# Rows 256 to 511 enter the first projection unscaled, and the scan's tables are asked for later

## The chip, the cores and the metric

The kernel runs on one core of a Trainium2 chip. A core has a matrix engine (PE in the profile), a vector engine (DVE), a scalar engine (ACT), a general engine (POOL) and a queue that mostly issues transfers (SP). Each takes its own instructions strictly in order; they meet through semaphores. The metric is the device time of one execution in microseconds (us). Executions of one kernel mostly agree within 0.3 per cent.

## What is computed

One layer of a hybrid encoder over 2048 rows of width 1024, all in float32:

```python
hn = rmsnorm(h, mix_norm_g)                       # per row: x * rsqrt(mean(x*x) + eps) * g
u, g_ssm, q, k, v, g_attn = split(hn @ w_in, 6)   # six times 512 columns
y_ssm = s5_branch(u, ...) * silu(g_ssm)           # diagonal complex scan, GELU, GLU
y_att = stick_breaking_branch(q, k, v, ...) * silu(g_attn)
h = h + concat([y_ssm, y_att]) @ w_out
h = h + sigmoid(rmsnorm(h) @ w_ple_gate) * (p @ w_ple_proj)
```

The reciprocal root of a row (its scale) is one number per row. It can be put on x before the product, or on the product behind it.

## The kernel before

Products keep float32 accuracy: each operand is split into a high and a low part (`split`, lines 505 to 508: ACT writes `hi`, DVE writes `lo = src - hi`), and three matmuls are made for each pair of blocks (`mm3`, lines 530 to 537).

The first phase (`phase_u`, line 540) makes u transposed: channels on partitions, rows along the free axis. It takes the rows in eight steps T of 256. A step needs `xt`, the transposed and split x, and the eight split blocks `w` of `w_in`'s first 512 columns; it makes 4 column tiles by 8 blocks by 3 = 96 matmuls of 128x256, into four banks `ps_u`.

- T = 0 (`load_plain`, line 546) reads a copy of x that the host has laid out transposed, so no transposes are needed and the scale isn't known when the products start. For each of four pairs of blocks, two transfers of 128 KB (one for each 128 rows), two splits, and two blocks of w (256 KB each, `load_w`, line 467, hi on ACT at line 485, lo on DVE at line 488) are asked for. `norms` (line 567) squares x in place on ACT, adds on POOL (line 571), sums over partitions with a matmul against ones (line 573), takes the power on POOL, and spreads the scale along the free axis as `e.row` with another matmul (line 579). The result in `ps_u` is multiplied by that row on DVE as it leaves the bank (line 627).
- T = 1 to 7 (`load_x`, line 582): the rows are loaded plainly, squared on ACT with a sum (line 590), the scale is worked out on DVE and POOL (`rms_rstd`, line 497), x is multiplied by it on ACT (line 592), transposed by PE into two banks `ps_x` (16 small transposes of 64x64 for each 128 rows), and split into `xt`. The result leaves `ps_u` by an ACT copy (line 629).

Every `xt` is also stored (`hn_d`), and the gate units (`gate_unit`, line 636) and the attention's projections (`attn_proj`, line 706) read it. Where it is unscaled (T = 0, rows 0 to 255) they multiply their products by the row's scale (`e.row` or `e.rs[i]`).

Beside this phase, `ssm_chain` (line 176) works out the scan's tables: a long string of small DVE instructions (`ex_`, `sc_`, `pr_`, `cm`, `tabs`, `pw`, `bb` in the profile). Its inputs come in seven transfers that POOL issues (lines 196, 198 and 205). `ssm_pack` (line 307) makes weights from them, four POOL and DVE instructions at a time; the first matmuls that use them come after the last step of u.

Nothing runs in program order. `arrange` (line 1525) takes all instructions with their dependencies, times them with a model of its own (`duration`, `list_schedule`), and writes out a fixed order for every engine, the best of six turns. Hints enter here: `e.first()` puts a group ahead, `e.mark(k)` names an instruction, and `e.later(k)` keeps a transfer in that plan behind the marked instruction. Any change thus renews the order of all engines over the whole kernel.

Tiles with one tag share a ring of buffers: `x` has four, `uq` (the results of u, and three of w's raw blocks ahead of them) has four.

Of the kernel before, what the change touches and what calls it, by code (L numbers as in the profile page):

```python
# [18 lines left out]
P = 128  # L19
# [30 lines left out]
HOLD = 2  # L50
ACT0 = True
MARK0, MARK1 = 7, 6
MATB = 1
# [122 lines left out]
def ssm_chain(e, keep, sm):  # L176
# [15 lines left out]

    dma = e.cdma
    ldt, lr, li = t("ldt"), t("lr"), t("li")
    for d, name in ((ldt, "log_dt"), (lr, "a_re"), (li, "a_im")):
        dma(d, e.small(name))
    dsk = R.dsk = kt("dsk", [G])
    dma(dsk[96:], e.small("d")[96:])

    bst = sm.tile([P, G, GH], F32, tag="bst", name="bst")  # L200
    bsw = sm.tile([P, G, GH], F32, tag="bsw", name="bsw")
    R.cts = kt("cts", [G, GH])
    R.ct2 = kt("ct2", [G, GH])
    for d, name in ((bst, "b"), (bsw, "b_turned"), (R.cts, "c"), (R.ct2, "c_turned")):
        dma(d, e.small(name).rearrange("p (g h) -> p g h", g=G))
    vs(nc, R.cts, R.cts, sgn, ALU.mult)
# [92 lines left out]
    for o, src, n in ((dec1, rho, KIN), (dec2, t1, MOUT), (tabs[:, :, NTAB - 1:].rearrange("p g n -> p n g"), rho, 1)):  # L299
        nc.vector.tensor_copy(o, src.unsqueeze(1).to_broadcast([P, n, G]))  # L300
        if n > 1:
            nc.vector.memset(o[:, 0], 0.0)
    dma(e.tb_d, tabs)
    return R
# [162 lines left out]
def load_w(e, blocks, width, scale, tag="w", pool=None, bufs=None, at=0, act=True, spare=None):  # L467

    nc = e.nc
    out = []  # L470
    for c, src in enumerate(blocks, at):
        t = (pool or e.wpool).tile([P, 2, width], F32R, tag=tag, name=f"w_{tag}", **({"bufs": bufs} if bufs else {}))
        hi, lo = t[:, 0], t[:, 1]
        if spare is None or c < STB + STA:
            raw = e.stage[c % len(e.stage)].tile([P, 512], F32, tag="wst", name="wst")[:, :width]
        else:
            raw = spare.tile([P, L, NCH // 2], F32, tag="uq", name="wst", bufs=4).rearrange("p j c -> p (j c)")[:, :width]
        if c == MARK0 and spare is not None:
            e.mark(0)
        e.wdma(raw.rearrange("p (k c) -> p k c", k=src.shape[1]) if len(src.shape) == 3 and src.shape[0] == P else raw, src)  # L480
        if scale is None:
            split(e, hi, lo, raw)
        else:
            if act:
                nc.scalar.activation(hi, raw, AF.Copy, scale=scale[:, c:c + 1])  # L485
# [54 lines left out]
def phase_u(e, pool, xp, chain):  # L540
# [5 lines left out]
    def load_plain(T):  # L546
        xt = xp.tile([P, 2, 2, NC8, P], F32R, tag="xg", name="xt", bufs=2)
        w = []
        for hf in range(2):
            plain.append(pool.tile([P, NC8, P], F32, tag="x", name="x", bufs=XB))  # L550
        for c in range(0, NC8, 2):
            cs = slice(c, c + 2)
            for hf in range(2):
                x = plain[2 * T + hf]
                nc.sync.dma_start(x[:, cs], e.xt[2 * T + hf, :, cs])
                split(e, xt[:, hf, 0, cs], xt[:, hf, 1, cs], x[:, cs])
            if T == 0:
# [8 lines left out]

    def norms(i):
        x, r = plain[i], e.rs[i]
        nc.scalar.activation(x, x, AF.Square)
        for n in (4, 2, 1):  # L570
            nc.gpsimd.tensor_tensor(x[:, :n], x[:, :n], x[:, n:2 * n], op=ALU.add)
        ps = e.bank("ps_row", "tr", "ssm")
        nc.tensor.matmul(ps[:, :1], x[:, 0], ones[:, :1], start=True, stop=True)
        vs(nc, r, ps[:, :1], 1.0 / DM, ALU.mult, EPS, ALU.add)
        nc.gpsimd.tensor_tensor(r, r, e.mhalf[:, :1], op=ALU.pow)
# [3 lines left out]
        nc.tensor.matmul(ps[:, :P], ones, d, start=True, stop=True)  # L579
        nc.scalar.activation(e.row[i // 2][:, i % 2 * P:i % 2 * P + P], ps[:, :P], AF.Copy)  # L580

    def load_x(T):
        xt = xp.tile([P, 2, 2, NC8, P], F32R, tag="xg", name="xt", bufs=2)
        for hf in range(2):
# [5 lines left out]
            nc.scalar.activation(jk, x, AF.Square, accum_out=ss)  # L590
            rs = rms_rstd(e, pool, ss, 1, DM, "x")
            nc.scalar.activation(x, x, AF.Copy, scale=rs)
            for h, ps in enumerate(turned(e, "ps_x", ("z0", "z1"), [x[:, c * P:(c + 1) * P] for c in range(NC8)])):
# [6 lines left out]
    with e.first():  # L600
        xts[0], w = load_plain(0)
        norms(0)
        norms(1)
        with e.later(0):
            xts[1] = load_x(1)
    prep = chain()
    for T in range(NT // 2):
# [4 lines left out]
        if T % 4 == 0:  # L612
            uq = [pool.tile([P, L, NCH // 2], F32, tag="uq", name="uq", bufs=4) for ct in range(4)]
        ps = [e.bank("ps_u", "w0", "w1", "o", "acc", *(("z0", "z1") if T < 1 else ()))[:, :256] for _ in range(4)]
        if T == 2:
            e.mark(T)
        for ct, c in [(ct, c) for c in range(NC8) for ct in range(4)] if T == 0 else [(ct, c) for ct in range(4) for c in range(NC8)]:
            if T == 0 and ct == 0 and c == MARK1:
# [4 lines left out]
        for ct in range(4):  # L623
            k0 = (T % 4) * n
            o, out = ps[ct].rearrange("p (c j) -> p j c", j=L), uq[ct][:, :, k0:k0 + n]
            if T < 1:
                vt(nc, out, o, e.row[T].rearrange("p (c j) -> p j c", j=L), ALU.mult)
            else:
                nc.scalar.activation(out, o, AF.Copy)
            if T % 4 == 3:  # L630
# [5 lines left out]
def gate_unit(e, pool, w, T, xt):  # L636
# [6 lines left out]
    for ct in range(4):  # L643
        o = e.bank("ps_sg", "o", "z0", "z1")[:, :256]
        for c in range(NC8):
            cs = slice(ct * P, (ct + 1) * P)
            mm3(e, o, (w[c][:, 0, cs], w[c][:, 1, cs]), (xt[:, :, 0, c], xt[:, :, 1, c]), c == 0, c == NC8 - 1)
        if T < 1:
            og = pool.tile([P, 256], F32, tag="sg", name="og", bufs=2)
# [56 lines left out]
def attn_proj(e, pool, A, i, xt=None):  # L706
# [8 lines left out]
    if len(e.q_banks) == 1:  # L715
        pq = e.bank("ps_qk", *e.q_banks)
        for c in range(NC8):
            mm3x(e, pq, (xt[:, 0, c], xt[:, 1, c]), (A.w[c][:, 0], A.w[c][:, 1]), c == 0, c == NC8 - 1)
        if i < 2:
            nc.scalar.activation(flat, pq[:, :384], AF.Copy, scale=e.rs[i])  # L720
# [4 lines left out]
    else:  # L725
# [7 lines left out]
        part = pool.tile([P, 512], F32, tag="part", name="part", bufs=1)  # L733
        if i < 2:
            nc.scalar.activation(part, pq[0], AF.Copy, scale=e.rs[i])
# [291 lines left out]
def hybrid_block_kernel(ctx: ExitStack, tc: tile.TileContext, x, xt, small, p, w_in, ssm_w_glu, w_out, w_ple_gate,  # L1027
# [36 lines left out]
    nc.vector.memset(e.mhalf, -0.5)  # L1064
    e.rs = [const(f"rs{i}", [P, 1]) for i in range(2)]

    def part(name):
        at = 0
        for q, n in SMALL:
            if q == name:  # L1070
                return small[:, at:at + n]
            at += n
# [10 lines left out]
    def late_consts():  # L1083
# [3 lines left out]
        gk = column("gk", 1)  # L1087
        vt(nc, e.gqk, e.gqk, gk, ALU.mult)

# [49 lines left out]
    gx = pool(left, "gx")  # L1139
    e.row = [gx.tile([P, 256], F32, tag=f"row{T}", name=f"row{T}") for T in range(1)]  # L1140
    early = ExitStack()
# [443 lines left out]
```

## Time and profile before

| | |
|---|---|
| three runs | 1561.94, 1563.83 and 4259.91 us |
| median | 1563.83 us |
| profiled execution | 1561.94 us, of which the span of the instructions is 1560.2 us |
| mean granted PE clock | 0.984 |
| instructions | 34921 |
| busy, share of the span | PE 95%, DVE 69%, ACT 60%, POOL 53% |

In a row of a timeline the columns are the start, the duration, the engine, the source line, the operation, `out<-in` with the names of the tiles, the shape and the count; in brackets stands how long the engine sat idle before it and what released it. In a row of a table by windows stand the window, its length, and then for each engine the busy time and the number of instructions, at the end the granted PE clock, the share of the DMA engines' time, and GB/s.

### The profile page before, as it was taken

Reading aid. Unit: us, or ns where it says so; the run is one execution under the profiler, and the core shown is the slowest. Engines: PE = TensorE matmul, PEld = TensorE weight load, DVE = VectorE, ACT = ScalarE, POOL = GpSimd, SP = SyncE. Lnnn points to the kernel's source line nnn. Section 1 sums busy time; section 2 is a strip of 40 time slices with the busy share of each in tenths; the row PEclk is TensorE's granted clock in tenths of the full one; section 3 lists DMA queues with packets and bytes.
Section 4 is the critical chain, followed back from the end, with each engine's and each line's share of the span. In section 5 each row is a group of like instructions: output and inputs, shape, how many; then the busy total and the mean of one; then the engine's idle time right before and its main releaser. Section 6 shows DMA issues by size and latency. Waiting matters only on the chain.

```text
span 1560.2 us, 34921 instructions
## 1 busy us (share of the span) xinstructions
PE 1480.4 (95%) x13116; PEld 1257.4 (81%) x13116; DVE 1073.6 (69%) x2052; ACT 938.7 (60%) x2076; POOL 819.2 (53%) x1038
## 2 busy tenths in 40 slices
PE   5999999999999999998999988999998999999998
PEld 5999999978888788887887876777776888777776
DVE  8944868867667876778867776666869556754444
ACT  5654445557577877677777777766765435633432
POOL 3241433445455665565656688765565654433433
PEclk8999999999999989999999988999999999999999
DMA  8777735565332412234323466763448645612211
GB/s 294 272 250 222 237 119 188 165 198 163 116 116 99 150 67 98 105 116 128 99 94 112 138 213 180 220 184 93 112 136 257 199 161 183 200 63 94 89 62 61
DMA packets 168969, 236.21 MB, mean 151 GB/s; under 512 B 63664, under 2 KB 110816, under 8 KB 157408
## 3 DMA queue, kind: packets, MB, share of 16 engines
q1 hardware_dynamic: 166416, 225.38, 44.7%
q0 software_dynamic: 2384, 8.59, 2.0%
q8 instruction: 104, 1.70, 0.4%
q14 instruction: 65, 0.53, 0.1%
HBM read 169.03 MB, written 64.90 MB: 150 GB/s over the span
## 4 chain that ended last, share of the span: by engine, by line
PE 74%; DVE 9%; ACT 5%; issue 4%; DMA 4%; POOL 3%; POOLq 0%; SPq 0%; ACTq 0%; DVEq 0%
PE ps_q L732 19%; PE ps_o L836 6%; PE ps_z L797 5%; PE ps_wt L520 4%; PE ps_g L701 3%; PE ps_g L703 3%; PE ps_g L702 3%; PE ps_h L702 3%; PE ps_h L703 3%; PE ps_h L701 3%; DVE px L813 2%; PE ps_sg L535 2%; PE ps_sg L536 2%; PE ps_sg L537 2%; DMA wst<-in_ssm_w_glu_dram 2%
## 5 line engine op out<-in xcount | busy, mean ns | idle before, releaser
L815 POOL TENSOR_TENSOR be<-be,px 128x512 f32<-128x512 f32 (+3 forms) x320 | 317.6, 998 | 224.3 <-DVE px L813 177.1
L813 DVE TENSOR_TENSOR_SCAN px<-px,ps_z 128x512 f32<-128x512 f32 (+3 forms) x320 | 340.2, 1086 | 108.6 <-ACT be L807 81.8
L732 PE MATMUL ps_q<-w_w,xt 64*128 64x512 f32 x2880 | 400.9, 404 | 6.6 <-DVE v L65 3.6
L732 PEld LDWEIGHTS ps_q<-w_w,xt 64*128 64x128 f32 x2880 | 294.5, 187 | 43.8 <-PE ps_z L797 7.2
L828 ACT ACTIVATE ws<-ps_wt 128x512 f32<-128x512 f32 (+3 forms) x320 | 165.0, 547 | 76.2 <-PE ps_wt L520 75.9
L802 ACT ACTIVATE px<-ps_z 128x512 f32<-128x512 f32 (+3 forms) x320 | 162.4, 538 | 67.6 <-PE ps_z L797 48.7
L807 ACT ACTIVATE be<-ps_z 128x512 f32<-128x512 f32 (+3 forms) x320 | 168.7, 554 | 1.3 <-PE ps_wt L520 1.2
L797 PE MATMUL ps_z<-k,q 64*128 64x512 f32 (+3 forms) x960 | 146.3, 385 | 15.9 <-DVE px L813 12.4
L836 PE MATMUL ps_o<-ws,v 128*64 128x128 f32 x2176 | 139.8, 281 | 0.9 <-ACT ws L828 0.9
L836 PEld LDWEIGHTS ps_o<-ws,v 128*64 128x64 f32 x2176 | 121.0, 140 | 19.1 <-issue 15.5
L520 PEld LDWEIGHTS ps_wt<-ident,be 64*128 64x128 f32 x2176 | 101.1, 142 | 36.6 <-issue 15.3
L797 PEld LDWEIGHTS ps_z<-k,q 64*128 64x128 f32 x960 | 94.9, 189 | 35.0 <-DVE px L813 18.2
L520 PE MATMUL ps_wt<-ident,be 64*128 64x64 f32 x2176 | 108.5, 229 | 13.4 <-POOL be L815 4.8
L1008 POOL TENSOR_TENSOR sg<-sg,h 128x512 f32<-128x512 f32 x32 | 44.9, 1414 | 114.6 <-DVE sg L65 114.6
L501 POOL TENSOR_TENSOR rs_qk<-rs_qk,mhalf 128x4 f32<-128x4 f32 x64 | 66.6, 1040 | 39.7 <-DVE rs_qk L72 38.8
L535 PE MATMUL ps_u<-xt,w_w 128*128 128x256 f32 x256 | 74.8, 294 | 8.1 <-ACT w_w L485 7.0
L65 DVE TENSOR_TENSOR yr<-sx,yr 128x512 fp32r<-128x512 f32 x64 | 53.6, 858 | 34.6 <-ACT yr L507 33.7
L537 PE MATMUL ps_u<-xt,w_w 128*128 128x256 f32 x256 | 74.3, 296 | 3.0 <-DVE w_w L76 3.0
L536 PE MATMUL ps_u<-xt,w_w 128*128 128x256 f32 x256 | 74.8, 293 | 0.7 <-DVE xt L65 0.7
L507 ACT ACTIVATE yr<-sx 128x512 fp32r<-128x512 f32 x64 | 39.3, 629 | 50.8 <-POOL sx L894 20.2
L811 POOL TENSOR_SCALAR_AFFINE_SELECT px<-px 128x128 f32<-128x128 f32 x128 | 41.2, 332 | 50.4 <-ACT px L802 49.1
L1002 ACT ACTIVATE sg<-sg,rs 128x512 f32<-128x512 f32 x24 | 17.4, 724 | 73.6 <-DVE sg L65 73.6
(418 smaller groups left out, 3674.5 us busy)
## 6 DMA issues: line engine op xcount, KB each, us to landing
xt<-hn SPq DMA_DIRECT2D x60, 1024.0 KB, 4.9
hn<-xt SPq DMA_DIRECT2D x16, 1024.0 KB, 5.5
h<-h SPq DMA_DIRECT2D x64, 256.0 KB, 3.6
wst<-in_w_in_dram SPq DMA_DIRECT2D x48, 256.0 KB, 3.3
xg<-hn SPq DMA_DIRECT2D x12, 1024.0 KB, 6.7
out_dram<-sg SPq DMA_DIRECT2D x32, 256.0 KB, 2.5
x<-in_x_dram SPq DMA_DIRECT2D x14, 512.0 KB, 5.3
h<-in_x_dram SPq DMA_DIRECT2D x28, 256.0 KB, 4.7
```

The source lines that it names most:

```text
L520: e.nc.tensor.transpose(ps[h][:, 64 * k:64 * k + 64], v[r], e.ident[r, r])
L535: mm(out, wh, xh, start=first, stop=False)
L536: mm(out, wh, xl, start=False, stop=False)
L537: mm(out, wl, xh, start=False, stop=last)
L732: nc.tensor.matmul(o, xt[r, a, c], A.w[c][r, b], start=c + s == 0, stop=c == NC8 - 1 and s == 2)
L797: nc.tensor.matmul(z[:, :n], q[half[h], a], A.k[ch][half[h], b, :n], start=s == 0, stop=s == 2)
L802: nc.scalar.activation(px[:, :n], z[:, :n], AF.Sigmoid, scale=-(HD ** -0.5))
L807: nc.scalar.activation(be[:, :n], z[:, :n], AF.Sigmoid, scale=HD ** -0.5)
L813: nc.vector.tensor_tensor_scan(rv, rv, z[:, :n][:, ::-1], initial=1.0 if carry[h] is None else carry[h], op0=ALU.mult, op1=ALU.bypass)
L815: nc.gpsimd.tensor_tensor(be[:, :n], be[:, :n], px[:, 1:n + 1], op=ALU.mult)
L828: nc.scalar.activation(dst, ps, AF.Copy)
L836: nc.tensor.matmul(po[half[h], :P], A.v[sb][:, h], w[:, h, b], start=sb == i, stop=sb == 0)
```

## The change

The steps T = 0 and T = 1 are now both unscaled (`RAW = 2`), so rows 256 to 511 lose the scaling on ACT ahead of their transposes, and have a row `e.row[1]` and two more `e.rs`. The host's transposed copy is laid out so that a pair of blocks of both halves is one piece of 256 KB. Step 0's raw x lives in two `uq` buffers and no longer in two `x` buffers; two raw blocks of w share one `uq` buffer. `norms` does both halves at once. The results of T = 0 and T = 1 leave their banks unscaled by ACT copies, and POOL multiplies them by the row in place. The scan's inputs come in three transfers on SP, one of them four times and two of them twice as wide as the parts were, held in the plan behind the seventh block of step 0 (mark 1) and behind the start of step 1 (mark 3). The list of banks for `ps_u` loses two entries in step 0. A product of two columns (`gqk`) moves from DVE to ACT.

```diff
+RAW = 2
 def ssm_chain(e, keep, sm):
-    for d, name in ((ldt, "log_dt"), (lr, "a_re"), (li, "a_im")):
-        dma(d, e.small(name))
-    dma(dsk[96:], e.small("d")[96:])
-    for d, name in ((bst, "b"), (bsw, "b_turned"), (R.cts, "c"), (R.ct2, "c_turned")):
-        dma(d, e.small(name).rearrange("p (g h) -> p g h", g=G))
+    with e.later(1):
+        nc.sync.dma_start(abd, e.small("log_dt", 4 * G).rearrange("p (k g) -> p k g", g=G))
+    with e.later(3):
+        for d, name in ((bs, "b"), (ct, "c")):
+            nc.sync.dma_start(d, e.small(name, 2 * G * GH).rearrange("p (k g h) -> p k g h", k=2, g=G))
...
 def load_w(e, blocks, width, scale, tag="w", pool=None, bufs=None, at=0, act=True, spare=None):
-            raw = spare.tile([P, L, NCH // 2], F32, tag="uq", name="wst", bufs=4).rearrange("p j c -> p (j c)")[:, :width]
+            n = (c - STB - STA) % 2
+            if n == 0:
+                e.half = spare.tile([P, L, NCH // 2], F32, tag="uq", name="wst", bufs=4).rearrange("p j c -> p (j c)")
+            raw = e.half[:, n * width:n * width + width]
...
     def load_plain(T):
-        for hf in range(2):
-            plain.append(pool.tile([P, NC8, P], F32, tag="x", name="x", bufs=XB))
+        for k in range(2):
+            plain.append(pool.tile([P, L, NCH // 2], F32, tag="uq", name="x", bufs=4).rearrange("p (k f u) c -> p k f (u c)", f=2, u=2))
         for c in range(0, NC8, 2):
             cs = slice(c, c + 2)
-            for hf in range(2):
-                x = plain[2 * T + hf]
-                nc.sync.dma_start(x[:, cs], e.xt[2 * T + hf, :, cs])
-                split(e, xt[:, hf, 0, cs], xt[:, hf, 1, cs], x[:, cs])
+            x = plain[c // 4][:, c % 4:c % 4 + 2]
+            nc.sync.dma_start(x, e.xt[:, cs])
+            hi, lo = (xt[:, :, k, cs].rearrange("p f c t -> p c f t") for k in range(2))
+            split(e, hi, lo, x)
...
-    def norms(i):
-        x, r = plain[i], e.rs[i]
-        nc.scalar.activation(x, x, AF.Square)
-        for n in (4, 2, 1):
-            nc.gpsimd.tensor_tensor(x[:, :n], x[:, :n], x[:, n:2 * n], op=ALU.add)
-        ps = e.bank("ps_row", "tr", "ssm")
-        nc.tensor.matmul(ps[:, :1], x[:, 0], ones[:, :1], start=True, stop=True)
-        vs(nc, r, ps[:, :1], 1.0 / DM, ALU.mult, EPS, ALU.add)
+    def row_of(i, ss):
+        r = e.rs[i]
+        vs(nc, r, ss, 1.0 / DM, ALU.mult, EPS, ALU.add)
         nc.gpsimd.tensor_tensor(r, r, e.mhalf[:, :1], op=ALU.pow)
         d = pool.tile([P, P], F32, tag="dg", name="dg", bufs=1)
         vs(nc, d, e.ident, r, ALU.mult)
         ps = e.bank("ps_row", "tr", "ssm")
         nc.tensor.matmul(ps[:, :P], ones, d, start=True, stop=True)
         nc.scalar.activation(e.row[i // 2][:, i % 2 * P:i % 2 * P + P], ps[:, :P], AF.Copy)
+    def norms():
+        a, b = plain
+        for x in plain:
+            nc.scalar.activation(x, x, AF.Square)
+        nc.gpsimd.tensor_tensor(a, a, b, op=ALU.add)
+        for n in (2, 1):
+            nc.gpsimd.tensor_tensor(a[:, :n], a[:, :n], a[:, n:2 * n], op=ALU.add)
+        for i in range(2):
+            ps = e.bank("ps_row", "tr", "ssm")
+            nc.tensor.matmul(ps[:, :1], a[:, 0, i], ones[:, :1], start=True, stop=True)
+            row_of(i, ps[:, :1])
...
     def load_x(T):
-            rs = rms_rstd(e, pool, ss, 1, DM, "x")
-            nc.scalar.activation(x, x, AF.Copy, scale=rs)
+            if T < RAW:
+                row_of(2 * T + hf, ss)
+            else:
+                rs = rms_rstd(e, pool, ss, 1, DM, "x")
+                nc.scalar.activation(x, x, AF.Copy, scale=rs)
...
-        ps = [e.bank("ps_u", "w0", "w1", "o", "acc", *(("z0", "z1") if T < 1 else ()))[:, :256] for _ in range(4)]
+        ps = [e.bank("ps_u", "w0", "w1", "o", "acc")[:, :256] for _ in range(4)]
+        if T == 1:
+            e.mark(3)
...
-            if T < 1:
-                vt(nc, out, o, e.row[T].rearrange("p (c j) -> p j c", j=L), ALU.mult)
-            else:
-                nc.scalar.activation(out, o, AF.Copy)
+            nc.scalar.activation(out, o, AF.Copy)
+            if T < RAW:
+                nc.gpsimd.tensor_tensor(out, out, e.row[T].rearrange("p (c j) -> p j c", j=L), op=ALU.mult)
...
 def gate_unit(e, pool, w, T, xt):
-        if T < 1:
+        if T < RAW:
 def attn_proj(e, pool, A, i, xt=None):
-        if i < 2:
+        if i < 2 * RAW:
...
-        vt(nc, e.gqk, e.gqk, gk, ALU.mult)
+        nc.scalar.activation(e.gqk, e.gqk, AF.Copy, scale=gk)
...
-            turned_x = _np.ascontiguousarray(a[0, :2 * P].reshape(2, P, NC8, P).transpose(0, 3, 2, 1))
+            turned_x = _np.ascontiguousarray(a[0, :2 * P].reshape(2, P, NC8, P).transpose(3, 2, 0, 1))
```

More of the change, by code (lines that the diff above doesn't have):

```diff
@@ L191, in ssm_chain @@
     vs(nc, nsgn, sgn, -1.0, ALU.mult)
-    dma = e.cdma
-    ldt, lr, li = t("ldt"), t("lr"), t("li")
-    for d, name in ((ldt, "log_dt"), (lr, "a_re"), (li, "a_im")):
-        dma(d, e.small(name))
-    dsk = R.dsk = kt("dsk", [G])
-    dma(dsk[96:], e.small("d")[96:])
[L200 to L203, printed above, removed]
-    for d, name in ((bst, "b"), (bsw, "b_turned"), (R.cts, "c"), (R.ct2, "c_turned")):
-        dma(d, e.small(name).rearrange("p (g h) -> p g h", g=G))
+    abd = kt("abd", [4, G])
+    bs = sm.tile([P, 2, G, GH], F32, tag="bs", name="bs")
+    ct = kt("cts", [2, G, GH])
+    with e.later(1):
[3 more added lines that the diff above has]
+            nc.sync.dma_start(d, e.small(name, 2 * G * GH).rearrange("p (k g h) -> p k g h", k=2, g=G))
+    ldt, lr, li, R.dsk = (abd[:, k] for k in range(4))
+    bst, bsw, R.cts, R.ct2 = bs[:, 0], bs[:, 1], ct[:, 0], ct[:, 1]
     vs(nc, R.cts, R.cts, sgn, ALU.mult)
@@ L302, in ssm_chain @@
             nc.vector.memset(o[:, 0], 0.0)
-    dma(e.tb_d, tabs)
+    e.cdma(e.tb_d, tabs)
     return R
@@ L601, in phase_u @@
         xts[0], w = load_plain(0)
-        norms(0)
-        norms(1)
+        norms()
         with e.later(0):
@@ L733, in attn_proj @@
         part = pool.tile([P, 512], F32, tag="part", name="part", bufs=1)
-        if i < 2:
+        if i < 2 * RAW:
             nc.scalar.activation(part, pq[0], AF.Copy, scale=e.rs[i])
@@ L1064, in hybrid_block_kernel, with part @@
     nc.vector.memset(e.mhalf, -0.5)
-    e.rs = [const(f"rs{i}", [P, 1]) for i in range(2)]
-    def part(name):
+    e.rs = [const(f"rs{i}", [P, 1]) for i in range(2 * RAW)]
+    def part(name, width=0):
         at = 0
@@ L1070, in part @@
             if q == name:
-                return small[:, at:at + n]
+                return small[:, at:at + (width or n)]
             at += n
@@ L1139, in hybrid_block_kernel @@
     gx = pool(left, "gx")
-    e.row = [gx.tile([P, 256], F32, tag=f"row{T}", name=f"row{T}") for T in range(1)]
+    e.row = [gx.tile([P, 256], F32, tag=f"row{T}", name=f"row{T}") for T in range(RAW)]
     early = ExitStack()
```

## The prediction

> **What bounds the kernel.** I read the page first, then a table of windows, then the engines' timelines where a window shows idle PE.
>
> ```profile
> span 1560.2 us, 34921 instructions
> PE 1480.4 (95%) x13116; PEld 1257.4 (81%) x13116; DVE 1073.6 (69%) x2052; ACT 938.7 (60%) x2076; POOL 819.2 (53%) x1038
> PE   5999999999999999998999988999998999999998
> ```
>
> PE is busy for 1480.4 of 1560.2 us, so a new order can take out 80 us at most, and what matmuls lose to a slow clock. The first of the 40 slices is the only one with PE at 5 tenths, and the changed code acts there. Next the windows, cut where the steps of u stand; after window and length come the busy times of PE, weight loads, DVE, ACT and POOL:
>
> ```profile
> 6.00:14.00 8.00, 6.47 (x38) 5.98 (x39) 8.00 (x48) 4.28 (x9) 0.24 (x1) 1.00 0.99 355
> 14.00:26.00 12.00, 8.70 (x63) 7.53 (x61) 11.21 (x55) 7.01 (x12) 5.37 (x6) 1.00 0.79 313
> 26.00:34.00 8.00, 3.63 (x39) 2.68 (x39) 8.00 (x37) 5.21 (x9) 2.46 (x5) 0.77 0.75 255
> 34.00:50.00 16.00, 15.28 (x124) 14.77 (x124) 14.80 (x85) 11.22 (x19) 3.13 (x4) 0.79 0.72 267
> 50.00:65.00 15.00, 14.48 (x139) 13.87 (x138) 14.89 (x70) 9.65 (x17) 2.31 (x3) 1.00 0.83 280
> 65.00:76.00 11.00, 9.58 (x98) 8.97 (x97) 10.94 (x20) 5.66 (x13) 4.09 (x5) 1.00 0.90 323
> 76.00:92.00 16.00, 13.85 (x122) 13.20 (x121) 13.78 (x12) 7.63 (x15) 12.59 (x9) 0.89 1.00 306
> 92.00:135.00 43.00, 43.00 (x398) 42.20 (x398) 9.86 (x17) 19.13 (x38) 11.14 (x9) 1.00 0.61 214
> 160.00:180.00 20.00, 20.00 (x175) 20.00 (x174) 19.43 (x28) 10.38 (x22) 10.79 (x5) 1.00 0.88 279
> ```
>
> From 6 to 76 us DVE is busy for 67.8 of 70 us: it is the bound there, and PE idles for 11.9 us. From 92 us on PE is full and DVE is busy for 9.86 of 43 us. So time that PE gains at the start is kept, and DVE has room for work that is put off. Then the steps themselves:
>
> ```profile
> 6.27 0.58 PE L535 MATMUL ps_u<-xt,w_w 128*128 128x256 f32 x1 [6.27 <-ACT w_w L485]
> 14.86 0.28 PE L537 MATMUL ps_u<-xt,w_w 128*128 128x256 f32 x1
> 14.97 0.28 PE L535 MATMUL ps_u<-xt,w_w 128*128 128x256 f32 x1
> 25.61 0.28 PE L537 MATMUL ps_u<-xt,w_w 128*128 128x256 f32 x1
> 28.15 0.71 PE L520 MATMUL ps_x<-ident,x 64*128 64x64 f32 x16 [0.38 <-ACT x L592]
> 31.24 1.11 PE L520 MATMUL ps_x<-ident,x 64*128 64x64 f32 x16 [1.67 <-ACT x L592]
> 33.53 0.58 PE L535 MATMUL ps_u<-xt,w_w 128*128 128x256 f32 x1 [1.17 <-ACT xt L507]
> 35.42 0.41 PE L535 MATMUL ps_u<-xt,w_w 128*128 128x256 f32 x1
> 35.64 0.41 PE L536 MATMUL ps_u<-xt,w_w 128*128 128x256 f32 x1
> 19.33 1.06 ACT L569 ACTIVATE x<-x 128x1024 f32<-128x1024 f32 x1 [3.28 <-DVE xt L65]
> 20.29 1.32 ACT L485 ACTIVATE w_w<-wst,gmix 128x512 fp32r<-128x512 f32 x2
> 26.95 1.15 ACT L592 ACTIVATE x<-x,rs_x 128x1024 f32<-128x1024 f32 x1 [2.17 <-POOL rs_x L501]
> 18.22 0.74 DVE L76 SCALAR_TENSOR_TENSOR w_w<-wst,gmix,w_w 128x512 fp32r<-128x512 f32 x1
> ```
>
> Step 0 runs from 6.27 to 25.9, 19.6 us, for 96 matmuls that start 0.11 to 0.12 us apart when nothing holds them (14.86 and 14.97), 11.5 us in all. What holds them is seen at 19.33: ACT's square waits 3.28 us for a split that DVE hasn't done, and the last blocks of w stand behind it on ACT until 20.29. DVE was busy with the scan's tables meanwhile. From 25.9 to 33.53 there is no product to make: step 1's transposes wait for ACT to scale x (line 592), so PE idles and then restarts slowly, 0.22 us from start to start (35.42 and 35.64). The window from 34 to 50 grants 0.79, that is (1 - 0.79) x 16 = 3.4 us of full speed lost.
>
> **The change part by part.** The rows for its prices:
>
> ```profile
> 10.00:12.00 2.00, 2.00 (x19) 1.00 1.05 395
> q0 software_dynamic: 448, 1.10, 5.4%
> L507 ACT ACTIVATE xt<-ps_x x28: 576/594/602, 28.9 to 119.1; 128x512 fp32r<-128x512 f32 x28
> L65 DVE TENSOR_TENSOR xt<-ps_x,xt x28: 670/681/695, 29.8 to 119.9; 128x512 fp32r<-128x512 f32 x28
> L579 PE MATMUL ps_row<-dg,ones x4: 275/311/377, 26.7 to 29.3; 128*128 128x128 f32 x4
> L65 DVE TENSOR_TENSOR uq<-ps_u,row x4: 566/568/592, 31.0 to 33.0; 128x256 f32<-128x256 f32 x4
> L629 ACT ACTIVATE uq<-ps_u x28: 362/384/417, 40.1 to 134.5; 128x256 f32<-128x256 f32 x28
> L346 PE MATMUL ps_pack<-cts,bn x48: 177/263/263, 135.7 to 177.0; 128*128 128x16 f32 x48
> 25.68 0.71 POOL L571 TENSOR_TENSOR x<-x 128x256 f32<-128x256 f32 x1
> 89.11 2.37 POOL L334 TENSOR_TENSOR stC<-stC,tm 128x1024 f32<-128x1024 f32 x1
> 20.48 4.68 POOL L571 TENSOR_TENSOR x<-x 128x512 f32<-128x512 f32 x4 [14.24 <-ACT x L569]
> 20.51 1.28 DVE L65 TENSOR_TENSOR pr_den<-pr_t,pr_t 128x32 f32<-128x32 f32 x1
> 78.06 7.86 DVE L65 TENSOR_TENSOR gq<-gq,gk 128x1 f32<-128x1 f32 x1
> 83.85 2.04 POOL L332 TENSOR_TENSOR stC<-pwr,cts 128x1024 f32<-128x1024 f32 x1
> 85.84 1.40 DVE L76 SCALAR_TENSOR_TENSOR w_w<-wst,gmix,w_w 128x512 fp32r<-128x512 f32 x2
> ```
>
> *Inputs.* Seven transfers leave POOL's queue and three enter SP's, later. 1.10 MB of table data no longer shares the first microseconds; at the 395 GB/s of the window from 10 to 12 us that is 2.8 us. What remains ahead of step 1 is 1 MB of x and 2 MB of w (8.0 us), then 1 MB for step 1 (2.7 us): in by about 14 us. SP issues four x pieces for eight; of its own queue nothing moves past a transfer that PE awaits, since the plan holds the table transfers behind the marks. The larger pieces change nothing that I can price: the first matmul needs both halves and the first block of w anyway.
>
> *DVE in step 0.* The tables leave the stretch before 16 us. The rest, 4 splits of 0.68 and 8 low parts of 0.74, is 8.6 us; ACT has 4 x 0.59 and 8 x 0.66, 7.6 us. Both keep ahead of PE, so step 0 becomes bound by PE: 11.5 us, and 1.5 for a cold start (an estimate: the first matmul takes 0.58 for 0.28, and some 16 of them at 0.21 for 0.12). It ends at 6.27 + 13.0 = 19.3.
>
> *Step 1.* The scaling (1.15 us twice, with its wait of 2.17) is gone, so the transposes need only the loaded x. They now run inside step 0: two times 0.71, 1.4 us of PE. The sums and rows of four halves instead of two make 12 small float32 passes of 0.31, which overlap: between 1.4 and 3.7 us, I take 1.5. The banks must be emptied by ACT (0.38) into `uq`, which holds squared x until POOL has added it: 2.37 for 1024 numbers, and the rest of four additions that took 4.68 for similar shapes, some 4.4 us behind squares that end near 14 us, thus 18.5 to 19. The margin to 19.3 is thin and I add 1.0 of waiting (0 to 3). Step 1 starts at 19.3 + 1.4 + 1.5 + 1.0 = 23.2 instead of 33.53: 10.3 us gained. The gap is then short, and the 3.4 us lost to the clock go too. **Sum: 13.7 us.**
>
> The clock may yet fall: no single wait that is shown between 26 and 34 us is over 1.67, and still that window has 0.77. So a string of short waits is enough here, and a poor hand-over at 20 us would cost about 3.4 us again; that is in the range.
>
> [...]
>
> *Tables later.* Of DVE's 67.8 us the splits and low parts take 3.4 (8 at 0.42, half a 128x512), 7.4 (10 at 0.74) and 10.9 (16 at 0.68), the banks 2.3 (4 at 0.57), packing 5; some 39 us are tables, an estimate. Put off to about 16 us, beside 2.7 us of splits in each step of 12.9 us (11.5 + 1.4), they end near 75, as before. They are needed at 135.7, or 122 with the gain: covered by 45 us, if the order lets the splits go first. If that cover fails, it is the third case below. Next to be late is step 2, whose x must be ready by 34.7: ACT has squares, scaling, splits and eight bank copies there, about 12 of 15 us.
>
> *POOL.* Eight multiplications of 0.71 are added, 5.7 us, and 2.3 us leave DVE. Nobody but the stores of u and later readers waits for them. They do hold DVE: 128 numbers took DVE 1.28 us at 20.51, under POOL's additions, and 7.86 at 78.06, until POOL's run of work ends at 85.89. For the tables that is time out of the 45 us.
>
> [...]
>
> *At nothing.* The shorter list of banks: the first four entries are the same, and step 0 takes four. [...] Four multiplications in the gate unit of step 1 at 0.41 to 0.57 on DVE, and scales read in the projections: PE is full there (20.00 of 20), though DVE has 19.43 in one window; 0 to 2 us, taken as 0.
>
> **The rivals.**
>
> *The stall from 65 to 92 goes too.* PE idles 3.6 us there and loses (1 - 0.89) x 16 = 1.8 to the clock, 5.4 together, behind DVE's wait at 78.06. For it: that instruction leaves DVE. [...] 1548.2 - 5.4 = 1542.8.
>
> *Half is given back.* POOL's additions or ACT's squares come late, step 1 starts 3 us later and cold (3.4 us), or the new order costs as much elsewhere. For it: a margin under 1 us. 1548.2 + 6.4 = 1554.6; if the edits don't act at all, 1561.9.
>
> *DVE's queue turns against PE: slower.* Tables that used to be done by 33 us now lie between the splits of steps 2 to 5 in one in-order queue, and each can be held by POOL: 4.4 us of additions, 5.7 of multiplications and four powers, 12 us. If the planner, which doesn't know the true waits, puts tables first, two steps start late and cold: 12 + 2 x 3.4 = 18.8 us lost against 13.7 gained, 1567; with four cold starts 1574. It decides once the splits are held for more than 13.7 us in all. Against: from 34 to 65 us DVE was just as full, and PE had 29.8 of 31.
>
> *The planner orders the later phases anew,* by more than 31 us one way or the other. The trace gives nothing for either sign: small chances.
>
> **How the numbers follow.** The sum is made against the profiled execution, 1561.94 us, which is 1.9 below the median of the runs: 1561.94 - 13.7 = 1548.2, so 1548. Chances: forecast 0.50 (1545 to 1553), the second stall too 0.15, half or all given back 0.19, DVE's queue 0.10, planner 0.03 faster and 0.03 slower. The range reaches from 1536, a start without the estimates' waits (1.0 and 1.5) and without the second stall, and 4 us for the planner, to 1566, which leaves out most of the slower case. Two per cent, about what a measurement of this kernel can tell from no change, is 31 us. All idle and slow PE time from 6 to 92 us is under 25 us, so faster by that much needs the planner: 0.04. Slower by that much: 0.04. Within: 0.92.
>
> **What would show it.** Right: a last product of step 0 near 20 us and a first of step 1 before 25; 0.12 us from start to start from about 10 us on; DVE's table instructions beginning after 15 us and the low parts of w done by then; the first `ps_pack` near 122. Wrong: PE waiting for `uq` or POOL's additions at 20 us; a granted clock under 0.9 between 20 and 40; `ps_x` or `ps_u` released by DVE's `xt` behind `cm` or `tabs` in steps 2 to 5; or a first `ps_pack` that is early while the end isn't.

## The result: the start is gained, and the end comes later

The changed kernel takes 1567.27 us (median of 20 runs, 1562.84 to 1570.38), the kernel before 1562.16 us beside it. The ratio is 1.0037, with a 95% interval of 1.0025 to 1.0049: slower by 0.4%, where a gain of 0.9% was forecast, and 1.3 us above the end of the range. The profiled execution took 1569.98 us, of which 1568.2 are the span. It is one of the slowest of the 20: the profiled spans lie 8.0 us apart, the medians 5.1.

The page of the changed kernel, its span, the busy times and PE's slices:

```profile
span 1568.2 us, 34924 instructions
PE 1489.2 (95%) x13120; PEld 1265.6 (81%) x13120; DVE 1072.9 (68%) x2049; ACT 936.5 (60%) x2077; POOL 818.5 (52%) x1035
PE   7889999969999999999999988999998999999998
```

PE's first slice rose from 5 tenths to 7, and the ninth, from 314 to 353 us, fell from 9 to 6. The timeline of PE in the changed kernel shows the start:

```profile
20.27 0.28 PE L538 MATMUL ps_u<-xt,w_w 128*128 128x256 f32 x1
...
23.71 0.69 PE L575 MATMUL ps_row<-dg,ones 128*128 128x128 f32 x2 [1.12 <-DVE dg L71]
24.06 0.56 PE L536 MATMUL ps_u<-xt,w_w 128*128 128x256 f32 x1
```

Step 0 ends at 20.27 + 0.28 = 20.55 us, and step 1's first product starts at 24.06 in place of 33.53. What became of these 9.5 us is read from a table of windows over the stages, first of the kernel before, then of the changed one:

```profile
0.00:40.00 40.00, 24.08 (x161) 21.36 (x162) 35.22 (x189) 23.17 (x39) 14.99 (x27) 0.88 0.80 291
40.00:134.00 94.00, 89.91 (x839) 86.84 (x839) 58.10 (x165) 49.04 (x90) 31.36 (x25) 0.98 0.74 254
134.00:240.00 106.00, 105.89 (x816) 101.50 (x815) 76.24 (x152) 54.94 (x129) 39.45 (x22) 1.00 0.62 191
240.00:280.00 40.00, 39.78 (x346) 39.61 (x345) 33.77 (x55) 20.76 (x47) 15.83 (x8) 1.00 0.63 196
280.00:320.00 40.00, 37.13 (x317) 36.61 (x317) 31.36 (x53) 20.12 (x45) 15.87 (x9) 1.00 0.47 145
320.00:360.00 40.00, 35.22 (x328) 29.04 (x328) 26.04 (x52) 24.93 (x67) 18.73 (x48) 0.96 0.60 200
```

```profile
0.00:40.00 40.00, 32.03 (x269) 30.75 (x269) 24.90 (x75) 27.82 (x50) 15.31 (x24) 0.96 0.88 341
40.00:134.00 94.00, 85.25 (x769) 82.22 (x769) 64.99 (x270) 42.36 (x79) 34.86 (x26) 0.96 0.70 235
134.00:240.00 106.00, 105.31 (x815) 101.08 (x814) 83.86 (x152) 53.83 (x123) 37.21 (x20) 1.00 0.61 184
240.00:280.00 40.00, 38.14 (x305) 37.07 (x304) 31.57 (x54) 19.77 (x45) 14.07 (x8) 0.96 0.67 218
280.00:320.00 40.00, 37.97 (x316) 37.67 (x315) 32.30 (x58) 21.99 (x49) 19.82 (x11) 0.97 0.45 133
320.00:360.00 40.00, 29.53 (x257) 24.02 (x258) 22.59 (x38) 21.20 (x53) 13.43 (x37) 0.82 0.54 174
```

Both kernels have the same matmuls but for four (13116 and 13120), so the count of those done is a rough clock of progress. Summed from the top, the changed kernel is ahead by 108 at 40 us (193 products of u in place of 121, which at 0.12 us are 8.6 us; most others are 32 small transposes, 1.4 us), by 38 at 134, by 37 at 240, behind by 4 at 280 and by 76 at 360. At 0.12 us each 76 are 9 us, about the 8.0 us between the spans. So nothing is lost after 360 us: the start is won, more than half of it is gone when u is done, and the rest and 9 us more go in two stretches, 240 to 280 and 320 to 360. In the last one PE idles 35.22 - 29.53 = 5.7 us more than before, and the granted clock is lower too, 0.82 in place of 0.96, which is another (0.96 - 0.82) x 40 = 5.6 us of full speed, a part of it while PE stood idle.

From the end of u to the attention, PE works on the scan's eight batches, with the gate units' products (`ps_sg`) and some projections (`ps_qk`) between them to fill its waits; then the attention begins. The rows of the tiles, each with the first and last start of its matmuls, before and after:

```profile
L537 PE MATMUL ps_sg<-xg,w_w x192: 278/283/368, 169.1 to 325.6; 128*128 128x256 f32 x192
...
L703 PE MATMUL ps_qk<-w_w,xg x32: 389/389/397, 190.6 to 229.6; 128*128 128x512 f32 x32
...
L458 PE MATMUL ps_y<-rot,stC x128: 269/275/376, 167.3 to 320.0; 128*128 128x127 f32 x128
...
L732 PE MATMUL ps_q<-w_w,xt x2880: 383/392/792, 332.4 to 1100.0; 64*128 64x512 f32 x192
```

```profile
L538 PE MATMUL ps_sg<-xg,w_w x192: 277/283/415, 163.4 to 314.4; 128*128 128x256 f32 x192
...
L714 PE MATMUL ps_qk<-w_w,xg x32: 389/389/397, 190.7 to 241.1; 128*128 128x512 f32 x32
...
L456 PE MATMUL ps_y<-rot,stC x128: 269/275/421, 168.0 to 328.2; 128*128 128x127 f32 x128
...
L743 PE MATMUL ps_q<-w_w,xt x2880: 384/392/771, 343.5 to 1107.9; 64*128 64x512 f32 x192
```

Before, the filler lasts longer (325.6) than the scan's last outputs (320.0). After, it runs out at 314.4, and the scan's outputs go on alone until 328.2. The main run of the attention's projections (`ps_q`) starts 11.1 us later. From there to the end of the span both take much the same: 1560.2 - 332.4 = 1227.8, and 1568.2 - 343.5 = 1224.7. What PE waits for in that stretch, the waits of PE from 140 to 360 us in the changed kernel:

```profile
PE ps_z L808 <- DVE px L824: 5.0, 1, 5.0
PE ps_o L847 <- ACT ws L839: 4.0, 3, 1.9
PE ps_y L456 <- DVE rot L66: 2.5, 2, 2.0
```

And the same waits in the kernel before:

```profile
PE ps_y L458 <- DVE rot L65: 1.7, 1, 1.7
PE ps_z L797 <- DVE px L813: 1.1, 1, 1.1
...
PE ps_o L836 <- ACT ws L828: 0.9, 1, 0.9
```

The columns are the wait with what ended it, the sum, the count and the longest. The 5.0 us at `px`, a step of the attention, are explained by ACT's timeline in the changed kernel:

```profile
330.07 0.60 ACT L458 ACTIVATE gsq<-ps_y 128x512 f32<-128x512 f32 x1 [2.04 <-DMA z<-gsq]
...
332.57 0.42 ACT L813 ACTIVATE px<-ps_z 128x128 f32<-128x128 f32 x2
```

ACT takes the last piece of the scan's output (`gsq`) at 330.07, behind a store that has to free its buffer, and only then the attention's first `px`. The scan's end has come so late that it meets the attention's start in the queues, and PE has nothing else. The scan is late from its fifth batch on. The turn of the fifth batch's inputs out of the bank on ACT, before and after:

```profile
241.75 0.60 ACT L396 ACTIVATE rot<-ps_b 128x512 f32<-128x512 f32 x1 [1.18 <-PE ps_b L395]
```

```profile
253.34 0.58 ACT L394 ACTIVATE rot<-ps_b 128x512 f32<-128x512 f32 x1
```

It comes 11.6 us later, and the `ps_qk` rows above show what stands ahead of it on PE: in the changed order these projections go on until 241.1 in place of 229.6. PE is not idle there, it does something else first.

### The profile page after: what moved, and what is told of

It reads as the page before. It is cut to its first block, busy times and chain, and to the rows that moved or that the text cites. A ratio compares the mean times of both kernels' runs of the same rounds, so it can differ in the third digit from the quotient of the medians.

```text
span 1568.2 us, 34924 instructions
## 1 busy us (share of the span) xinstructions
PE 1489.2 (95%) x13120; PEld 1265.6 (81%) x13120; DVE 1072.9 (68%) x2049; ACT 936.5 (60%) x2077; POOL 818.5 (52%) x1035
## 5 line engine op out<-in xcount | busy, mean ns | idle before, releaser
L743 PE MATMUL ps_q<-w_w,xt 64*128 64x512 f32 x2880 | 406.7, 405 | 9.2 <-DVE v L66 5.7
L808 PE MATMUL ps_z<-k,q 64*128 64x512 f32 (+3 forms) x960 | 150.7, 389 | 16.2 <-DVE px L824 15.5
L521 PEld LDWEIGHTS ps_wt<-ident,be 64*128 64x128 f32 x2176 | 104.7, 142 | 31.0 <-issue 11.6
L808 PEld LDWEIGHTS ps_z<-k,q 64*128 64x128 f32 x960 | 96.5, 191 | 38.6 <-DVE px L824 23.2
L502 POOL TENSOR_TENSOR rs_qk<-rs_qk,mhalf 128x4 f32<-128x4 f32 x64 | 66.2, 1035 | 38.5 <-DVE rs_qk L73 37.7
```

What stands on the lines that cost most here:

```text
L521: e.nc.tensor.transpose(ps[h][:, 64 * k:64 * k + 64], v[r], e.ident[r, r])
L743: nc.tensor.matmul(o, xt[r, a, c], A.w[c][r, b], start=c + s == 0, stop=c == NC8 - 1 and s == 2)
L808: nc.tensor.matmul(z[:, :n], q[half[h], a], A.k[ch][half[h], b, :n], start=s == 0, stop=s == 2)
```

## The experiments

Three theories went into the runs. **A**: the tables, asked for later, keep DVE from the splits of steps 2 to 5, and PE loses there what it gained. **B**: as step 1 is unscaled, the gate unit takes a second buffer of the ring `sg` for each column tile (`og`), which slows the stage of the batches. **C**: neither; the planner renews the order of the whole kernel at any edit, and it came to a poor one for the stage of the batches. All times are medians; each ratio is to the kernel before, measured beside it on the same chip. The ratio is taken from the runs and not from the two medians, so it differs a little from their quotient (most in e11_og_psum_t20: 0.9952, and 1551.06 / 1561.57 = 0.9933).

| kernel | us | before | ratio, 95% | step 1's first product | fifth batch turned | first `ps_q` |
|---|---|---|---|---|---|---|
| kernel before | 1562.16 | | | 33.53 | 241.75 | 332.4 |
| changed kernel | 1567.27 | 1562.16 | 1.0037 [1.0025, 1.0049] | 24.06 | 253.34 | 343.5 |
| e1_raw1 | 1563.75 | 1560.06 | 1.0024 [1.0010, 1.0039] | 26.34 | 247.97 | 336.0 |
| e2_gate1_free | 1562.59 | 1560.06 | 1.0017 [1.0005, 1.0029] | 24.58 | 246.76 | 336.0 |
| e3_tables_early | 1569.23 | 1560.06 | 1.0056 [1.0038, 1.0075] | 30.33 | 257.06 | 343.2 |
| e4_only_late | 1555.60 | 1560.06 | 0.9971 [0.9960, 0.9982] | 28.14 | 237.36 | 328.3 |
| e5_og_psum | 1557.88 | 1561.41 | 0.9970 [0.9955, 0.9985] | 24.11 | 244.35 | 329.5 |
| e6_before_og_psum | 1568.69 | 1561.41 | 1.0037 [1.0017, 1.0056] | 33.56 | 251.41 | 342.3 |
| e7_after_20_turns | 1563.68 | 1561.41 | 1.0010 [0.9996, 1.0024] | 23.93 | 250.67 | 340.4 |
| e8_row_on_dve | 1565.50 | 1561.41 | 1.0032 [1.0014, 1.0049] | 29.95 | 251.95 | 341.8 |
| e9_after_ord | 1553.14 | 1561.57 | 0.9946 [0.9926, 0.9966] | 24.15 | 241.50 | 327.6 |
| e10_before_ord | 1567.81 | 1561.57 | 1.0043 [1.0023, 1.0064] | 33.54 | 250.16 | 339.4 |
| e11_og_psum_t20 | 1551.06 | 1561.57 | 0.9952 [0.9933, 0.9971] | 24.33 | 246.12 | 330.8 |

The three columns on the right are starts in the profiled executions, one for each kernel, which can lie some us off the median (e3_tables_early: 1564.48 us, median 1569.23). The time follows the last of them and not the first: the four kernels whose first `ps_q` is at 330.8 us or earlier take 1551 to 1558 us, the kernel before with 332.4 some 1562, the two with 336.0 about 1563, and the six in which it comes at 339 us or later take 1564 to 1569, whether step 1 started at 24, 30 or 33.5.

### One part undone

**e1_raw1**: the changed kernel, with step 1 scaled on ACT as before.

```diff
-RAW = 2
+RAW = 1
```

> The changed kernel with only step 0 unscaled; step 1 is scaled on ACT as in the kernel before. Tables late, larger pieces, POOL multiplications of step 0 stay. Theory A (the late tables keep DVE from the splits of steps 2 to 5 and cost the gain): stays slow, 1565 to 1570, first product of step 1 after 28 us. Theory B (an unscaled step 1 makes the gate unit take two of the two sg buffers for each column tile, which slows the stage of the scan's batches): the loss goes, 1558 to 1563, last ps_y near 320 us as before. Theory C (the planner's new order alone, whatever the edit): anywhere from 1556 to 1572, with no relation to A or B.

Measured: 1.0024 [1.0010, 1.0039]. Step 1 starts 2.3 us later than in the changed kernel (26.34, where A has it after 28), and the time is under the 1565 of A. B has the last `ps_y` about right (322.3), and its time is missed by 0.75 us. That speaks for B or C, but weakly: the interval overlaps that of the changed kernel.

**e2_gate1_free**: the changed kernel, where the gates of rows 256 to 511 are not multiplied by their scale, so no second buffer is taken for them.

```diff
 def gate_unit(e, pool, w, T, xt):
-        if T < RAW:
+        if T < 1:
```

> The changed kernel, but the gate unit of step 1 doesn't multiply its product by the row's scale, so the gates of rows 256 to 511 are of another size; the start is untouched. A: 1567 as the change, since tables and splits are the same. B: 1558 to 1563, last ps_y 5 us or more before 328. C: any.

Measured: 1.0017 [1.0005, 1.0029]. The last `ps_y` is at 321.9, as B has it, and the time lies in B's range; C allows both. The 0.2% that seems to come back is not clear of noise, since the interval overlaps that of the changed kernel.

**e3_tables_early**: the changed kernel, with the three transfers of the tables issued by POOL at once, without their marks.

```diff
-    with e.later(1):
-        nc.sync.dma_start(abd, ...)
-    with e.later(3):
-            nc.sync.dma_start(d, ...)
+    nc.gpsimd.dma_start(abd, ...)
+            nc.gpsimd.dma_start(d, ...)
```

> The changed kernel with the three table transfers asked for at once by POOL, nothing else. A: 1550 to 1560, PE no longer waits 2.9 us for a split at 56 us, the first table instruction on DVE near 5 us, but step 0 slower. B: 1565 to 1570, the last ps_y at 326 us or later. C: any.

Measured: 1.0056 [1.0038, 1.0075], no better than the changed kernel. Step 0 now ends at 25.7 us, as before the change (25.9), and step 1 starts at 30.33. A would have it at 1550 to 1560; A misses by 9 us, though this run, too, has an order of its own. The run also shows what the late tables are worth at the start: 30.33 - 24.06 = 6.3 us.

**e4_only_late**: the kernel before, with the three wide transfers on SP behind marks 1 and 3, and nothing else of the change.

```diff
+    with e.later(1):
+        nc.sync.dma_start(abd, e.small("log_dt", 4 * G)...)
+    with e.later(3):
+            nc.sync.dma_start(d, e.small(name, 2 * G * GH)...)
```

> The kernel before with only the three later table transfers of the change. A: slower than before, 1564 to 1570, since the tables lie among the later splits and nothing is gained by unscaled rows. B: not slower, 1555 to 1562: step 0 runs faster without tables on DVE, and the gate units are as before. C: any.

Measured: 0.9971 [0.9960, 0.9982], faster than both kernels. Here step 0 ends at 19.5 us, step 1 still waits for its scaled x until 28.14, and the gain stays to the end. A, which has it at 1564 or more, misses a second time: late tables alone don't make a kernel slow.

**e8_row_on_dve**: the changed kernel, with the results of steps 0 and 1 scaled on DVE out of the bank, as before the change, so POOL's eight multiplications are gone.

```diff
-            nc.scalar.activation(out, o, AF.Copy)
             if T < RAW:
-                nc.gpsimd.tensor_tensor(out, out, e.row[T]..., op=ALU.mult)
+                vt(nc, out, o, e.row[T]..., ALU.mult)
+            else:
+                nc.scalar.activation(out, o, AF.Copy)
```

> The changed kernel with the results of steps 0 and 1 multiplied by the row on DVE as they leave the bank, as before, and not by ACT and POOL. [...] A, B: 1565 to 1570, as they lie elsewhere, and the start loses 1 to 3 us because the banks wait for the row. C: any.

Measured: 1.0032 [1.0014, 1.0049]. The timeline of PE at step 1's first product:

```profile
28.27 0.79 PE L575 MATMUL ps_row<-dg,ones 128*128 128x128 f32 x2 [0.38 <-DVE dg L71]
29.53 0.77 PE L575 MATMUL ps_row<-dg,ones 128*128 128x128 f32 x2 [0.47 <-DVE dg L71]
29.95 0.56 PE L536 MATMUL ps_u<-xt,w_w 128*128 128x256 f32 x1
```

The banks now wait for the rows, so step 1 starts 29.95 - 24.06 = 5.9 us later. The end does not move with it: 1565.5 against 1567.27. The multiplications on POOL are what lets the banks go early. In the changed kernel three DVE instructions of 128x32, started at 27.67 to 29.27 us beside four of them (26.82 to 30.12), take 0.84 to 0.92 us each, and one at 30.07, behind these four, takes 0.18: some 2 us of DVE. Taking the multiplications away doesn't bring the time back. The 1 to 3 us expected at the start are missed.

### The same edit on both kernels

**e5_og_psum** and **e6_before_og_psum**: the changed kernel and the kernel before, with the gate's product scaled in its bank and no copy of it.

```diff
-            og = pool.tile([P, 256], F32, tag="sg", name="og", bufs=2)
-            vt(nc, og, o, e.row[T], ALU.mult)
-            o = og
+            vt(nc, o, o, e.row[T], ALU.mult)
```

> The changed kernel with one edit: the gate unit's scaled product is written back into its bank on DVE, so that it takes no sg buffer; all results as in the change. A: 1567. B: the loss goes and part of the start's gain is kept, 1552 to 1562. C: any of 1556 to 1572.

> The kernel before with the same edit of the gate unit (it touches step 0's gate unit alone). B: a small gain or none, 1556 to 1563. C: the order is drawn anew, and a kernel of which nothing got worse can be several us slower, 1556 to 1570. A says nothing.

Measured: 0.9970 [0.9955, 0.9985] on the changed kernel, 1.0037 [1.0017, 1.0056] on the kernel before. By B the edit can only free a buffer. The one is 9.4 us faster by it (1567.27 to 1557.88), and the other, in which it frees buffers as well, 7.3 us slower (1561.41 to 1568.69; by the ratio 5.8). The kernel before has no scaled copy left with this edit, and its fifth batch is turned at 251.41 all the same. So a late fifth batch doesn't need B's copies, and B, which hit with the one kernel and missed with the other, cannot be the cause by itself. What both kernels have in common is that the planner made a new order.

**e7_after_20_turns**: the changed kernel, and the planner takes the best of 20 turns.

```diff
-def best_order(ops, pre, soft, length, mode, rows, turns=6):
+def best_order(ops, pre, soft, length, mode, rows, turns=20):
```

> The changed kernel, only that the planner takes the best of 20 turns for 6, so another order of the same instructions. A and B: 1564 to 1570, as they don't hang on the order. C: 1558 to 1565 or another difference of 3 us or more.

Measured: 1.0010 [0.9996, 1.0024]. The same instructions in another order are 3.6 us faster, as C allows; A and B, at 1564 or more, miss by 0.3 us only.

### The order alone

If C holds, an edit that changes no instruction must move the time, and can move it in either direction. **e9_after_ord** and **e10_before_ord** are the changed kernel and the kernel before with two lines exchanged in the loop that writes the batches of the scan. The two lines share no bank and no ring of buffers, so only the place from which the planner takes its first ranks differs.

```diff
-        xg = gate_unit(e, gx, wgate, T, xts.get(T))
         if last is not None:
             list(last)
+        xg = gate_unit(e, gx, wgate, T, xts.get(T))
         last = g
```

> The changed kernel with two lines of its loop over the scan's batches exchanged: the second half of the previous batch is written ahead of the next gate unit instead of behind it. Instructions, tiles and transfers are the same; only the place in the program from which the planner takes its first ranks differs. Theory B (the scaled copy of the gate's product takes a second buffer and slows the stage of the batches) and theory A (late tables) leave the time where the changed kernel has it, about 1567 us, within 0.2%. Theory C (the order that the planner comes to for the stage of the batches decides, and the change merely drew a poor one) lets the time move by several us with nothing else changed: I expect 1554 to 1561 us, the scan's fifth batch turned earlier than the 253.3 us of the changed kernel, the last ps_y nearer to 320 than to 328 us.

> The kernel before with the same two lines exchanged. Theories A and B say nothing about it: 1562 us, within 0.2%. Theory C: several us in either direction with the same instructions; I expect 1565 to 1572 us, slower than the kernel before by about as much as the change was, so that of two kernels with this order the changed one is the faster. If both this kernel and the exchanged changed kernel stay at their old times, theory C falls.

Measured: 0.9946 [0.9926, 0.9966] and 1.0043 [1.0023, 1.0064]. With the lines exchanged the changed kernel is at 1553.14 us and the kernel before at 1567.81: the sign of the change has turned. The first is 0.9 us under the range of C, the second within it. A and B have the first at 1567: it keeps the late tables and the copies of the gate's product, and it is 14 us faster. The changed kernel with exchanged lines, first the busy times of its page, then its windows:

```profile
PE 1482.3 (95%) x13120; PEld 1258.3 (81%) x13120; DVE 1069.5 (69%) x2049; ACT 935.7 (60%) x2077; POOL 820.9 (53%) x1035
```

```profile
0.00:40.00 40.00, 32.25 (x262) 30.59 (x263) 24.00 (x74) 27.38 (x49) 15.29 (x24) 0.91 0.88 333
40.00:134.00 94.00, 87.91 (x795) 84.91 (x794) 63.65 (x273) 43.86 (x84) 32.49 (x26) 0.96 0.70 236
134.00:240.00 106.00, 103.72 (x795) 98.80 (x794) 82.37 (x156) 54.31 (x127) 40.22 (x21) 1.00 0.65 201
240.00:280.00 40.00, 38.00 (x328) 37.80 (x327) 39.39 (x60) 21.47 (x49) 20.60 (x10) 1.00 0.55 164
280.00:320.00 40.00, 40.00 (x346) 40.00 (x345) 28.96 (x55) 22.24 (x47) 11.64 (x8) 1.00 0.56 169
320.00:360.00 40.00, 35.53 (x342) 29.13 (x341) 25.77 (x53) 24.97 (x68) 22.13 (x52) 0.91 0.58 194
```

Each engine has the very counts of the changed kernel (13120, 2049, 2077, 1035). The start is the same too: 262 matmuls by 40 us, 269 there. Of the 101 that it is then ahead of the kernel before, 57 are left at 134 us and 61 at 360, where the changed kernel is 76 behind. Its tiles in the stage of the batches, and the fifth batch on ACT:

```profile
L538 PE MATMUL ps_sg<-xg,w_w x192: 278/283/365, 163.2 to 320.4; 128*128 128x256 f32 x192
...
L714 PE MATMUL ps_qk<-w_w,xg x32: 389/389/398, 188.6 to 228.1; 128*128 128x512 f32 x32
...
L456 PE MATMUL ps_y<-rot,stC x128: 269/275/376, 163.6 to 314.9; 128*128 128x127 f32 x128
```

```profile
241.50 0.60 ACT L394 ACTIVATE rot<-ps_b 128x512 f32<-128x512 f32 x1 [1.25 <-PE ps_b L393]
```

The projections end at 228.1, the fifth batch is turned at 241.50, and the filler (320.4) outlasts the scan's outputs (314.9): the same picture as in the kernel before, 5 us earlier at its end. In the kernel before with exchanged lines the loss has another place, and the timeline of PE has the longest wait of it in one row:

```profile
189.20 0.77 PE L701 MATMUL ps_qk<-w_w,xg 128*128 128x512 f32 x1 [5.02 <-DVE b_en L65]
```

PE waits 5.02 us for DVE's work on a batch. So a poor order has no one wait that belongs to it.

**e11_og_psum_t20**: the product scaled in its bank, and 20 turns.

> The changed kernel with the gate's product of the unscaled rows scaled in place in its bank (no copy of it, as in the run that gave 1557.88) and the planner taking 20 turns instead of 6. Theory C alone: the in-place scaling is worth nothing by itself, so an order sought longer gives any time from 1555 to 1565. Theory B: the copy's buffer was the cost, so the time stays at 1558, within 0.2%. If B and C both hold a part, 1553 to 1558, faster than both kernels.

Measured: 0.9952 [0.9933, 0.9971]. The median of 1551.06 us is under all three ranges; the ratio gives 0.9952 x 1561.57 = 1554 us, in the range for both. The interval overlaps those of e5_og_psum and of e9_after_ord, so it doesn't tell B from C. A part of B thus stays open. Of the five kernels in which the gates of rows 256 to 511 keep their copy, four have the first `ps_q` at 340 us or later; of the four changed kernels without that copy (e1_raw1, e2_gate1_free, e5_og_psum, e11_og_psum_t20) none has it after 336.0. The copy may make a poor order likelier; that isn't shown, and e9_after_ord (327.6) shows that it doesn't force one. With e9_after_ord it is the fastest kernel here; both beat the kernel before by 0.5%.

## Why the prediction was wrong

**The start was right.** Step 0 ended at 20.55 us (19.3 forecast), step 1's first product came at 24.06 (23.2), 9.5 us earlier than before (10.3). The shares are as worked out: the late tables alone (e4_only_late) end step 0 at 19.5, and without them (e3_tables_early) it goes on to 25.7, with DVE busy for 32.72 of the first 40 us (35.22 before, 24.90 after). (The tables' inputs were eight transfers, not seven as said above; their 1.10 MB are right.)

**The clock's 3.4 us came back only by half.** The windows of the changed kernel for that place and the next:

```profile
14.00:26.00 12.00, 10.44 (x95) 9.74 (x94) 7.23 (x15) 9.72 (x19) 7.39 (x8) 0.91 1.02 417
26.00:34.00 8.00, 7.77 (x69) 7.39 (x69) 4.85 (x12) 4.27 (x12) 4.73 (x7) 0.92 0.85 332
...
50.00:65.00 15.00, 11.75 (x114) 11.08 (x113) 14.12 (x82) 8.81 (x17) 2.77 (x3) 0.89 0.60 205
```

They lose (1 - 0.91) x 12 + (1 - 0.92) x 8 = 1.7 us of full speed at the hand-over, so the start gave 9.5 + 1.7 = 11.2 us of the 13.7. The count agrees: at 50 us the changed kernel is 96 matmuls ahead, 11.5 us at 0.12.

**DVE's queue did turn against PE, at a smaller price.** In 50 to 65 us PE's busy time fell from 14.48 to 11.75 at a clock of 0.89, that is 2.7 us and (1 - 0.89) x 15 = 1.7 us of full speed. The wait behind it, in PE's timeline:

```profile
56.64 0.27 PE L521 MATMUL ps_x<-ident,x 64*128 64x64 f32 x1 [2.92 <-DVE xt L66]
...
94.06 0.38 PE L536 MATMUL ps_u<-xt,w_w 128*128 128x256 f32 x1 [3.23 <-ACT uq L638]
```

The split that PE awaits at 56.64 stood behind tables on DVE, as the slower rival had it, but once and for 2.92 us, not for 12 and two cold starts. It stays in e9_after_ord (2.90 us), which is the faster kernel all the same, so it decides nothing. That this rival's sum, 1567, is the measured time is luck: it adds up 12 us of held splits and two cold starts of 3.4 us, where PE's transposes waited 4.9 us for splits from 40 to 134 us, and 3.8 before the change. The wait of 3.23 us for a bank that ACT empties is of the order: 0.18 us in e9_after_ord.

**The step that failed** is "time that PE gains at the start is kept", with its term for the planner, "4 us". It was argued from PE being full from 92 us on. A full PE in the old trace shows that the old order fills PE; it doesn't show that the new order will, and that every edit renews the order was known from the planner. Of 10 us in hand at 40 us the new order kept about 4 at 134, then spent these and 9 more in the stage of the batches. The first part of that loss isn't peculiar to this order: the six kernels with this start (262 to 269 matmuls by 40 us, 101 to 108 ahead) have 38 to 57 left at 134. Why a part goes while u is made in all six is not settled; the waits for splits (4.9 and 3.8 us) differ too little for it. The second part is the order's, as e9_after_ord shows. In e9_after_ord, with the same instructions, 61 matmuls, 7 us, are still in hand at 360, and the span is 1560.2 - 1553.1 = 7.1 us shorter. Two rivals named the new order: one at over 31 us, with small chances, the other, by which half is given back, as one cause among several of 6.4 us. Against the forecast 1567.27 - 1548.2 = 19 us were lost, between the two. The pairs of this study, each with the same edit on both kernels, differ by +5.1 us (as they are), -10.8 (scaled in the bank) and -14.7 (lines exchanged). The first is a slower kernel. The last is near the 13.7 us of the forecast, but pairs so far apart don't confirm it. How often the planner draws which order for this change can't be told from three pairs.

**The signs that were named.** First product of step 1 before 25: right. A clock under 0.9 between 20 and 40 us, a sign of being wrong, came too (0.50 from 24 to 27), at the 1.7 us above. First `ps_pack` near 122: wrong, 136.0, and 134.3 before (135.7 is the first of another form of it); in e9_after_ord it is at 128.9. Tables after 15 us: they began at 27.67 and ended at 89, not at 75. DVE's 7.86 us at `gq` are gone, as the rival on the second stall hoped, but PE's idle time from 65 to 92 us fell only from 3.6 to 2.8 us, and nothing of it is seen at the end. None of these signs looks at the stage in which the time was lost.

## What to carry to other kernels

Where a planner renews the order of the whole program, a local edit is measured together with a new order of everything behind it, and here that order was worth 14 us on the changed kernel (1567.27 and 1553.14) and 6 on the kernel before, as much as the edit. Price it as a term of its own, from the kernel's own runs: make an edit that changes no instruction, on both kernels, and see how far the time moves before you judge the change by one pair. And follow progress through the stages (matmuls done by a given time, the first start of each tile), so that a gain at the start is not taken for a gain at the end.

## What the runs showed of the hardware

The clock fell at the shorter hand-over as well. In the changed kernel, cut into windows of 1 us, PE's busy time and granted clock at step 1's start:

```profile
22.00:23.00 1.00, 0.38 (x2) 0.30 (x2) 0.68 (x4) 1.00 (x4) 0.77 (x2) 1.00 1.02 409
23.00:24.00 1.00, 0.29 (x2) 0.29 (x3) 1.00 (x3) 1.00 (x3) 0.81 (x2) 0.93 1.03 431
24.00:25.00 1.00, 1.00 (x6) 1.00 (x6) 0.54 (x2) 1.00 (x4) 0.00 (x0) 0.50 1.04 438
```

Two microseconds in which PE is busy for 0.67, with no idle stretch above 1.12, are followed by a clock of 0.50 until 27 us. In the 3.5 us from 20.5 to 24.0 PE was busy for 1.94. That the loss to the clock goes when the gap is short was the author's estimate; here 1.7 us of full speed were lost behind a stretch that is only partly idle.
